# S5 mixer: states kept by pairs of groups, products of 64 rows, inputs in larger pieces, and one staging place moved

## The chip, the core and the metric

The kernel runs on one core of a Trainium2 chip. Its time is the device time of one execution in microseconds (us). Before the change three executions took 2720.01, 2723.41 and 2724.05 us; the median is 2723.41 us. Engines are named as the profile names them: PE multiplies matrices (PEld loads its weights), DVE works on vectors, ACT applies functions, POOL is a second, general vector engine, and SP issues most of the DMAs.

## What is computed

One inference step of a two-layer decoder on 1024 prompt tokens and 64 tokens of 8 samples, 1088 columns in all. Layer 0 is an S5 state-space mixer with cross-attention to a memory and a squared-ReLU MLP; layer 1 is attention with forgetting, the same memory attention and MLP. The part that is changed most is the S5 mixer: 48 groups of 16 channels, each with 64 complex states.

```python
def step(carry, u_t):                       # one chunk of 128 tokens
    hr, hi = carry
    bur = jnp.einsum("ntgc,gpc->ntgp", u_t, bb_re)
    bui = jnp.einsum("ntgc,gpc->ntgp", u_t, bb_im)
    ...
    _, _, sr, si = lax.associative_scan(_ssm_combine, (ar, ai, bur, bui), axis=1)
    y = (jnp.einsum("ntgp,gcp->ntgc", sr, c_re) - jnp.einsum("ntgp,gcp->ntgc", si, c_im)
         + d * u_t)
...
z = jax.nn.gelu(y)
out = z * jax.nn.sigmoid(z @ w_glu + b_glu)
```

The MLP is `h = relu(x @ w_up); (h * h) @ w_down` with 4096 hidden rows.

## The kernel before

Most products split a float32 operand into a rounded high part and a low part (`split`, L216: ACT copies the high part at L221, DVE or POOL subtracts it at L222) and multiply three times (`mm3`, L211). The 1088 columns are worked in four pieces of 272. Each engine works off its own queue in order; a planner that runs when the kernel is built sets the order in each queue from the order of the program and its own estimate of costs, so neighbouring parts of the program are interleaved. Memory is handed out as places that are used one after the other: `setA` (four units of 2176 words), `setB`, `setC`, and a flexible area with `sq0`, `rs0`, `nt0`. A piece of the program that writes a place waits until everyone who read it is done, DMAs too.

**Opening.** The keys and values of the memory are computed (L869 to L895; the values of one half pass through the place `u3`, from which L894 and L895 send them out), `norm0` (L905) normalizes the four pieces, where `rms_apply` (L278) gives every second split to POOL, and DVE works out the tables of S5 (L938 to L1046). ACT and POOL copy the powers of the transition matrix into `W1` and `W2`, half of the partitions at a time (L1003 to L1009).

**`prep(q)`** (L1049, six times, 8 groups each) makes the matrices of eight groups: `bb` (DVE, L1061 to L1066, 64 elements per partition), its block form `bd`, the powers `pt` (DVE, L1082 to L1087), their transposes `P` (PE, L1091), the output matrices `Q` (POOL, L1104 to L1109) and the short-range kernel, which goes through HBM and comes back as `M`.

**`phases_of(u)`** (L1131, twelve times) makes the phases by which a chunk's states are turned back and forth (DVE L1139 to L1141, POOL L1142 to L1144). **`s5_in`** (L1147) multiplies the normalized pieces with `w_in0`; the result goes through HBM and comes back as `U`.

**`s5_unit`** (L1167, twelve units of four groups): PE makes P·U in products of 64 output rows, groups 2a and 2a+1 of a pair on the lower and upper 64 partitions, real and imaginary part in separate banks. DVE multiplies by the phases (L1185, L1186), combines (L1188, L1189) and scans (L1193); POOL (L1195) and DVE (L1196) multiply the scanned states by the phases again into `A` and `B`. Then the layout changes: DVE (L1201) and POOL (L1202) assemble `Sg`, in which the 128 partitions hold the real and the imaginary states of one group. PE adds M·U and Q·Sg for each group in one bank, ACT applies Gelu (L1214), and the result goes out to HBM (L1215). The loop over units (L1225) runs nine units ahead of the dense layer of the memory queries (L1243), and the last three beside it.

**The MLP** (`mlp`, L504, once per layer) makes the hidden rows in 16 steps j; `to_hidden` (L528) combines and splits them, and SP sends them to HBM (`hops`, `hcnv`, issued at L526). Four places `hl`/`hl4` (L511, L512; for the last step L605) stage what is sent. The down product works in blocks (b, d); the first one (L639 on) writes its sums into `H5`, which lies over the same `setA` (L610): block d = 0 covers the words 0 to 1087 of each unit, block d = 1 the words 1088 to 2175. The sums are written by DVE at L627.

## Time and profile before

| | us |
|---|---|
| median of three executions | 2723.41 |
| the profiled execution | 2729.51 |
| its span, first to last instruction | 2727.7 |
| PE busy (mean granted clock 0.978) | 2564.0 |
| DVE busy | 1959.2 |
| POOL busy | 1213.1 |

The opening and the S5 mixer take the first 268 us of the span. Up to there PE is busy 213 us, DVE 233 us and POOL 163 us. The two MLPs' down products start at about 872 and 2371 us.

### The profile page before, as it was taken

Reading aid. Unit: us, or ns where it says so; the run is one execution under the profiler, and the core shown is the slowest. Engines: PE = TensorE matmul, PEld = TensorE weight load, DVE = VectorE, ACT = ScalarE, POOL = GpSimd, SP = SyncE. Lnnn points to the kernel's source line nnn. Section 1 sums busy time; section 2 is a strip of 40 time slices with the busy share of each in tenths; the row PEclk is TensorE's granted clock in tenths of the full one; section 3 lists DMA queues with packets and bytes.
Section 4 is the critical chain, followed back from the end, with each engine's and each line's share of the span. In section 5 each row is a group of like instructions: output and inputs, shape, how many; then the busy total and the mean of one; then the engine's idle time right before and its main releaser. Section 6 shows DMA issues by size and latency. Waiting matters only on the chain.

```text
span 2727.7 us, 54053 instructions
## 1 busy us (share of the span) xinstructions
PE 2564.0 (94%) x20369; PEld 2392.2 (88%) x20369; DVE 1959.2 (72%) x3406; ACT 1256.6 (46%) x2612; POOL 1213.1 (44%) x1119
## 2 busy tenths in 40 slices
PE   6888899999998999999999999999989999899998
PEld 5777779899998999999889867777989999899998
DVE  8898665988886777794323278886588788677776
ACT  5433444566663222244322367775366665322224
POOL 4576310323321799842310455651032222179984
PEclk8999899999999999999999999999999999999999
DMA  6445352266558567443476889986226656866741
GB/s 200 106 104 146 117 163 76 91 242 243 229 228 324 232 254 277 178 167 102 150 259 222 268 290 308 304 294 218 91 87 244 236 227 234 318 242 244 285 169 67
DMA packets 242283, 561.66 MB, mean 206 GB/s; under 512 B 54053, under 2 KB 129382, under 8 KB 224614
## 3 DMA queue, kind: packets, MB, share of 16 engines
q1 hardware_dynamic: 212646, 548.50, 56.7%
q10 hardware_dynamic: 28864, 8.92, 1.4%
q8 instruction: 161, 2.64, 0.4%
q0 software_dynamic: 512, 0.79, 0.1%
q14 instruction: 100, 0.82, 0.1%
HBM read 386.19 MB, written 171.93 MB: 205 GB/s over the span
## 4 chain that ended last, share of the span: by engine, by line
PE 41%; DVE 18%; POOL 10%; DMA 10%; issue 6%; ACT 4%; SPq 0%; POOLq 0%; ACTq 0%; DVEq 0%
PE banks L209 39%; DMA hops<-plain 5%; DVE rounded L222 5%; POOL plain L630 4%; DVE plain L222 4%; PE banks L1667 1%; POOL plain L416 1%; DMA rounded<-hmid 1%; DVE plain L578 1%; POOL plain L646 1%; ACT plain L221 1%; POOL plain L422 1%; DMA hcnv<-plain 1%; POOL plain L417 1%; DMA plain<-fpast 1%
## 5 line engine op out<-in xcount | busy, mean ns | idle before, releaser
L209 PE MATMUL banks<-rounded 128*128 128x272 f32 (+3 forms) x11168 | 1552.6, 295 | 72.8 <-ACT rounded L221 18.3
L209 PEld LDWEIGHTS banks<-rounded 128*128 128x128 f32 x11168 | 1456.7, 191 | 120.3 <-ACT rounded L221 21.1
L221 ACT ACTIVATE rounded<-plain 128x512 fp32r<-128x512 f32 (+5 forms) x573 | 379.8, 676 | 637.5 <-PE banks L209 449.3
L222 DVE TENSOR_TENSOR rounded<-plain,rounded 128x512 fp32r<-128x512 f32 (+4 forms) x518 | 502.8, 976 | 121.7 <-ACT rounded L221 120.3
L209 PE MATMUL banks<-mlp,rounded 128*128 128x272 f32 x3816 | 516.8, 290 | 12.2 <-DVE plain L627 4.8
L209 PEld LDWEIGHTS banks<-mlp,rounded 128*128 128x128 f32 x3816 | 493.8, 189 | 17.2 <-DVE plain L627 5.3
L416 POOL TENSOR_TENSOR plain<-plain 128x512 f32<-128x512 f32 x60 | 103.9, 1731 | 705.9 <-DVE rounded L222 705.9
L630 POOL TENSOR_TENSOR plain<-plain,flex 128x544 f32<-128x544 f32 x192 | 289.8, 1520 | 37.7 <-DVE plain L629 34.8
L222 DVE TENSOR_TENSOR plain<-plain 128x544 fp32r<-128x544 f32 x212 | 171.1, 820 | 69.9 <-ACT plain L221 69.1
L221 ACT ACTIVATE plain<-plain 128x544 fp32r<-128x544 f32 x212 | 136.7, 650 | 111.6 <-DMA hops<-plain 99.1
L629 DVE TENSOR_TENSOR plain<-banks,plain 128x544 f32<-128x544 f32 x192 | 137.9, 718 | 50.3 <-PE banks L209 46.8
L422 POOL TENSOR_TENSOR plain<-plain 128x512 f32<-128x512 f32 x60 | 98.3, 1639 | 63.0 <-DVE rounded L222 62.6
L209 PE MATMUL banks<-flexr,rounded 128*128 128x272 f32 x816 | 114.5, 290 | 4.0 <-DVE flexr L222 4.0
L209 PE MATMUL banks<-layer 128*32 128x256 f32 (+3 forms) x1152 | 111.9, 368 | 5.5 <-DVE layer L1770 1.7
L579 ACT ACTIVATE plain<-plain 128x544 f32<-128x544 f32 (+1 forms) x136 | 83.2, 613 | 66.0 <-DVE plain L578 65.5
L209 PEld LDWEIGHTS banks<-flexr,rounded 128*128 128x128 f32 x816 | 107.8, 191 | 4.4 <-DVE flexr L222 4.4
L222 POOL TENSOR_TENSOR rounded<-plain,rounded 64x512 fp32r<-64x512 f32 (+2 forms) x55 | 77.9, 1424 | 67.1 <-ACT rounded L221 61.9
L222 POOL TENSOR_TENSOR rounded<-flex,rounded 128x544 fp32r<-128x544 f32 (+7 forms) x100 | 65.9, 668 | 83.7 <-ACT rounded L221 71.0
L578 DVE TENSOR_TENSOR plain<-banks,plain 128x544 f32<-128x544 f32 (+1 forms) x136 | 90.5, 666 | 11.8 <-PE banks L209 11.2
L222 DVE TENSOR_TENSOR rounded<-banks,rounded 128x512 fp32r<-128x512 f32 (+2 forms) x136 | 86.0, 637 | 13.1 <-ACT rounded L221 11.3
L221 ACT ACTIVATE rounded<-banks 128x512 fp32r<-128x512 f32 (+2 forms) x136 | 75.1, 559 | 42.0 <-PE banks L1667 29.3
L418 POOL TENSOR_TENSOR plain<-plain 128x512 f32<-128x512 f32 x60 | 91.7, 1528 | 2.8
(365 smaller groups left out, 3227.0 us busy)
## 6 DMA issues: line engine op xcount, KB each, us to landing
hops<-plain SPq DMA_DIRECT2D x196, 544.0 KB
rounded<-hops SPq DMA_DIRECT2D x66, 1088.0 KB
plain<-in_cache_kT SPq DMA_DIRECT2D x128, 384.0 KB
layer<-in_cache_v SPq DMA_DIRECT2D x128, 384.0 KB
mlp<-hops SPq DMA_DIRECT2D x32, 1088.0 KB
plain<-in_w_up SPq DMA_DIRECT2D x32, 1024.0 KB
plain<-in_w_down SPq DMA_DIRECT2D x28, 1024.0 KB
plain<-in_xT SPq DMA_DIRECT2D x8, 1088.0 KB
```

Source lines behind the costliest of these rows:

```text
L209: PE.matmul(out, a, b, start=first, stop=last)
L221: S.activation(H, src, AF.Copy)
L222: return e.tensor_tensor(L, src, H.bitcast(F32), op=ALU.subtract)
L416: G.tensor_tensor(a22, a21, a22, op=ALU.add)
L417: G.tensor_tensor(a21, a11, a21, op=ALU.subtract)
L418: G.tensor_tensor(a11, a22, a11, op=ALU.subtract)
L422: G.tensor_tensor(a12, a12, a11, op=ALU.subtract)
L578: V.tensor_tensor(x, ps, u, op=ALU.add)
L579: S.activation(x, x, AF.Relu)
L629: V.tensor_tensor(h, ps, h, op=ALU.add)
L630: G.tensor_tensor(h, h, u, op=ALU.add)
L646: G.tensor_tensor(hc, hc, hr[:, m, :], op=ALU.add)
```

## The change

*Staging.* For the last step of an MLP the fourth staging place is words 1088 to 2175 of `setA[1]` in place of words 0 to 1087.

*Tables.* `Wr` and `Wi` hold the powers of pairs of groups, real and imaginary part apart, on all 128 partitions: 16 copies on ACT in place of 32 half ones on ACT and 32 on POOL. All of `s5_b` comes in one DMA into `u3`, and `bb` is worked out once for all six q in six DVE instructions of 384 elements. `s5_c` comes in two DMAs for each q. The phases are made for two units at a time, 512 elements per instruction. The initial states come once and are copied by ACT.

*Unit.* `Sg` is gone. DVE's last multiplication is split in two, the second one with a factor of -1. For each group PE adds M·U and four products of 64 rows: real and imaginary matrix by `B`, real and imaginary matrix by `A`; the two groups of a pair read the lower and the upper 64 partitions and write two banks. The Gelus of a unit come after all of its products.

```diff
-                hl4 = [hl.p[1], hl.p[0], hl.p[2], setA[1].sub(0, 1088)]
+                hl4 = [hl.p[1], hl.p[0], hl.p[2], setA[1].sub(1088, 1088)]
...
-    Pr, Er = late.ring(3, 1024), late.ring(3, 512)
-    abr, xring = late.ring(2, 1024), late.ring(2, 512)
+    Pr, Er = late.ring(3, 1024), Ring([late.words(1024), sq0.sub(0, 1024)])
+    abr, xring = late.ring(2, 1088), late.ring(2, 512)
...
-    W1, W2 = pp([128, 8, 48]), pp([128, 8, 48])
+    Wr, Wi = pp([128, 24, 8]), pp([128, 24, 8])
     for t in range(8):
-        for h in range(2):
-            hs = slice(64 * h, 64 * h + 64)
-            r, i = are[hs, 7 - t, :], aim[hs, 7 - t, :]
-            S.activation(W1[0:64, t, h::2], r, AF.Copy)
-            S.activation(W1[64:128, t, h::2], i, AF.Copy, scale=-1.0)
-            G.tensor_copy(W2[0:64, t, h::2], i)
-            G.tensor_copy(W2[64:128, t, h::2], r)
+        S.activation(Wr[:, :, t], are[:, 7 - t, :], AF.Copy)
+        S.activation(Wi[:, :, t], aim[:, 7 - t, :], AF.Copy)
...
+    bb = pp([128, 6, 2, 4, 16])
+    bc = u3.at([128, 6, 2, 4, 16])
+    SY.dma_start(out=bc, in_=I["s5_b"].rearrange("q p r a c -> p q r a c"))
+    tb = rs0.at([128, 6, 4, 16])
+    crb, cib = (x.rearrange("p (q a) -> p q a", a=4)[:, :, :, None].broadcast_to([128, 6, 4, 16]) for x in (cr, ci))
+    V.tensor_tensor(bb[:, :, 0], crb, bc[:, :, 0], op=ALU.mult)
+    V.tensor_tensor(tb, cib, bc[:, :, 1], op=ALU.mult)
+    V.tensor_tensor(bb[:, :, 0], bb[:, :, 0], tb, op=ALU.subtract)
...
-        bb = bbr([128, 2, 4, 16])
-        tb = tbr([128, 4, 16])
-        crb = cr[:, prs, None].broadcast_to([128, 4, 16])
-        cib = ci[:, prs, None].broadcast_to([128, 4, 16])
-        V.tensor_tensor(bb[:, 0], crb, bc[:, 0], op=ALU.mult)
-        V.tensor_tensor(tb, cib, bc[:, 1], op=ALU.mult)
-        V.tensor_tensor(bb[:, 0], bb[:, 0], tb, op=ALU.subtract)
...
+        cc = ccr([128, 2, 4, 16])
         for h in range(2):
             hs = slice(64 * h, 64 * h + 64)
-            for r in range(2):
-                S.activation(bd[64 * r:64 * r + 64, :, h, 16 * h:16 * h + 16], bb[hs, r], AF.Copy)
+            SY.dma_start(out=cc[hs], in_=I["s5_c"][q][hs].rearrange("p r (a h) c -> p h r a c", h=2)[:, h])
+            S.activation(bd[hs, :, :, 16 * h:16 * h + 16], bb[hs, q], AF.Copy)
+
+        S.activation(cc[:, 1], cc[:, 1], AF.Copy, scale=-1.0)
...
-        G.tensor_tensor(Q, wt(W1), ct(0), op=ALU.mult)
...
+            G.tensor_tensor(Q[:, i], wt(Wr), ct(i), op=ALU.mult)
             tq = tqr([128, 4, 8, 16])
-            G.tensor_tensor(tq, wt(W2)[:, gs], ct(1)[:, gs], op=ALU.mult)
-            G.tensor_tensor(Q[:, gs], Q[:, gs], tq, op=ALU.subtract)
-        S.activation(c0[0:64], cc[0:64, 0], AF.Copy)
-        S.activation(c0[64:128], cc[64:128, 1], AF.Copy, scale=-1.0)
+            G.tensor_tensor(tq, wt(Wi), ct(1 - i), op=ALU.mult)
+            G.tensor_tensor(Q[:, i], Q[:, i], tq, op=ALU.subtract if i else ALU.add)
...
-        V.tensor_tensor(B, X, Es[:, None].broadcast_to(s5b), op=ALU.mult)
-        Sg = sgr([128, 4, 136])
-        Sv = Sg.rearrange("p (a h) j -> p h a j", h=2)
+        V.tensor_tensor(B[:, 0], X[:, 0], Es, op=ALU.mult)
+        V.scalar_tensor_tensor(B[:, 1], X[:, 1], -1.0, Es, op0=ALU.mult, op1=ALU.mult)
...
+        S.activation(As[:, :, :, 128:136], hsm[:, :, 2 * u:2 * u + 2, :], AF.Copy)
+        Y = yr([128, 4, 136])
+
+        o = [ybank([128, 2, 136]) for _ in range(2)]
+        for i in range(2):
+            for h in range(2):
+                g = 4 * hh + 2 * i + h
+                mm(o[h][:, i], M[:, g, :], U[:, g, :], True, False)
+            for r, x, n, last in ((0, B[:, 1], 128, False), (1, B[:, 0], 128, False),
+                                  (0, As[:, 0], 136, False), (1, As[:, 1], 136, True)):
+                for h in range(2):
+                    hs = slice(64 * h, 64 * h + 64)
+                    mm(o[h][:, i, 0:n], Q[hs, r, 2 * hh + i], x[hs, i], False, last)
         for h in range(2):
-            hs = slice(64 * h, 64 * h + 64)
-            V.tensor_tensor(Sv[0:64, h, :, 0:128], A[hs, 0], B[hs, 1], op=ALU.subtract)
-            G.tensor_tensor(Sv[64:128, h, :, 0:128], A[hs, 1], B[hs, 0], op=ALU.add)
-        hc = slice(2 * u, 2 * u + 2)
-        G.tensor_tensor(h9[:, 0, hc, 0:1], A[:, 0, :, 127:128], B[:, 1, :, 127:128], op=ALU.subtract)
-        G.tensor_tensor(h9[:, 1, hc, 0:1], A[:, 1, :, 127:128], B[:, 0, :, 127:128], op=ALU.add)
-        S.activation(Sg[:, :, 128:136], h0[:, 4 * u:4 * u + 4, :], AF.Copy)
-        Y = yr([128, 4, 136])
-        for i in range(2):
-            ps2 = ybank([128, 272])
-            for g in (2 * i, 2 * i + 1):
-                o = ps2[:, 136 * (g % 2):136 * (g % 2) + 136]
-                mm(o, M[:, 4 * hh + g, :], U[:, 4 * hh + g, :], True, False)
-                mm(o, Q[:, 4 * hh + g, :], Sg[:, g, :], False, True)
-            S.activation(Y[:, 2 * i:2 * i + 2, :].rearrange("p b j -> p (b j)"), ps2, AF.Gelu_apprx_tanh)
+            S.activation(Y[:, h::2, :], o[h], AF.Gelu_apprx_tanh)
```

The order on DVE in the opening, in the second piece of the normalization (L272 to L285 in both; `prep_150` holds the tables, L1082 to L1087 before are the powers of `prep(0)`; L1033 and L1036 are the new instructions for `bb`, L1130 a phase). Before:

```order
104 L1063 TENSOR_TENSOR flex_69<-flex_69 128x64 [waits DVE_49]
105 L1140 TENSOR_TENSOR prep_150<-prep_150 128x256 [waits Activation_49]
106 L1065 TENSOR_TENSOR flex_69<-prep_150 128x64 [waits DVE_49]
107 L1082 TENSOR_TENSOR prep_150<-prep_150,flex_69 128x4x128
108 L1066 TENSOR_TENSOR flex_69<-flex_69 128x64 [waits DVE_49]
109 L1083 TENSOR_TENSOR prep_150<-prep_150,flex_69 128x512 [waits DVE_49]
110 L1085 TENSOR_TENSOR prep_150<-prep_150,flex_69 128x4x128
111 L1062 TENSOR_TENSOR flex_69<-prep_150 128x64 [waits DMAHW0_49]
112 L1084 TENSOR_TENSOR prep_150<-prep_150 128x4x128 [waits DVE_49]
113 L272 TENSOR_TENSOR flex_69<-flex_69 128x272 [waits Activation_49]
114 L1064 TENSOR_TENSOR flex_69<-prep_150 128x64 [waits DVE_49,Activation_49]
115 L1086 TENSOR_TENSOR prep_150<-prep_150,flex_69 128x512 [waits DVE_49]
```

After:

```order
103 L272 TENSOR_TENSOR flex_69<-flex_69 128x272 [waits Activation_49]
104 L273 SCALAR_TENSOR_TENSOR flex_69<-banks,flex_69 128x272 [waits DVE_49]
105 L274 TENSOR_SCALAR flex_69<-flex_69 128x272 [waits DVE_49]
106 L275 TENSOR_TENSOR flex_69<-flex_69 128x272 [waits DVE_49]
107 L285 SCALAR_TENSOR_TENSOR flex_69<-plain,flex_69 128x272 [waits DVE_49]
108 L285 SCALAR_TENSOR_TENSOR flex_69<-plain,flex_69 128x272 x3
109 L285 SCALAR_TENSOR_TENSOR flex_69<-plain,flex_69 128x272 [waits Pool_49]
110 L285 SCALAR_TENSOR_TENSOR flex_69<-plain,flex_69 128x272
111 L222 TENSOR_TENSOR rounded<-flex_69,rounded 128x544 [waits Activation_49]
112 L1033 TENSOR_TENSOR prep_150<-prep_150 128x6x64 [waits DMAHW0_49]
113 L1036 TENSOR_TENSOR prep_150<-prep_150 128x6x64
114 L1130 TENSOR_TENSOR plain<-prep_150 128x512 [waits DVE_49]
```

The normalization of this piece stood behind and between the instructions of `prep(0)`; these now come after all four pieces, and the piece holds the first two instructions on `bb`, which wait for a DMA.

The order on PE around the products of the first unit (64x136 is P·U; before, flex 128x136 is Q·Sg and rounded 128x136 is M·U; after, plain is Q by `B`, 128x128, and by `A`, 128x136; 128x272 is the dense layer). Before:

```order
60 L209 MATMUL banks<-rounded 128x272 x52
61 L209 MATMUL banks<-flex_69,plain 128x136
62 L209 MATMUL banks<-rounded 128x136
63 L209 MATMUL banks<-flex_69,plain 128x136 x2
64 L209 MATMUL banks<-rounded 128x136
65 L209 MATMUL banks<-flex_69,plain 128x136
66 L209 MATMUL banks<-rounded 128x272 x18
```

After:

```order
57 L209 MATMUL banks<-rounded 128x272 x32
58 L209 MATMUL banks<-plain 128x128 x4
59 L209 MATMUL banks<-plain 128x136 x4
60 L209 MATMUL banks<-rounded 128x136 x2
61 L209 MATMUL banks<-plain 128x128 x4
62 L209 MATMUL banks<-plain 128x136 x4
63 L209 MATMUL banks<-rounded 128x272 x22
```

Two products of a pair with `Sg` have become eight of 64 rows that stand in a row, and the dense layer's products follow the first unit as before.

The order on DVE at the start of the first down product of the first MLP, with what each instruction waits for (L627 writes `H5`; L445 and L449 combine sums; DMAHW are semaphores of DMAs). Before:

```order
1067 L445 TENSOR_TENSOR flex_8251<-banks,flex_8251 128x544 [waits PE_49]
1068 L222 TENSOR_TENSOR rounded<-plain,rounded 128x512 [waits Activation_49]
1069 L222 TENSOR_TENSOR rounded<-plain,rounded 128x512 [waits PE_49,Activation_49]
1070 L627 TENSOR_TENSOR plain<-banks,flex_8251 128x2x272 [waits DMAHW0_49,DVE_49]
1071 L449 TENSOR_TENSOR flex_8251<-banks,flex_8251 128x544
1072 L627 TENSOR_TENSOR plain<-banks,flex_8251 128x2x272 [waits PE_49]
1073 L627 TENSOR_TENSOR plain<-banks,flex_8251 128x2x272 [waits DMAHW1_49,DVE_49]
1074 L449 TENSOR_TENSOR flex_8251<-banks,flex_8251 128x544
1075 L627 TENSOR_TENSOR plain<-banks,flex_8251 128x2x272 [waits PE_49]
```

After:

```order
1009 L445 TENSOR_TENSOR flex_8234<-banks,flex_8234 128x544 [waits PE_49]
1010 L222 TENSOR_TENSOR rounded<-plain,rounded 128x512 [waits Activation_49]
1011 L627 TENSOR_TENSOR plain<-banks,flex_8234 128x2x272 [waits DVE_49,PE_49]
1012 L449 TENSOR_TENSOR flex_8234<-banks,flex_8234 128x544
1013 L627 TENSOR_TENSOR plain<-banks,flex_8234 128x2x272 [waits DVE_49,PE_49]
1014 L449 TENSOR_TENSOR flex_8234<-banks,flex_8234 128x544
1015 L222 TENSOR_TENSOR rounded<-plain,rounded 128x512 [waits Activation_49]
1016 L627 TENSOR_TENSOR plain<-banks,flex_8234 128x2x272 [waits PE_49] x2
```

The two writes that waited for DMAs wait for DVE and PE alone.

## Rows read from the trace of the kernel before

**Rows 1.** The page, part 4: the share of each engine on the chain that ended last.
```profile
PE 41%; DVE 18%; POOL 10%; DMA 10%; issue 6%; ACT 4%; SPq 0%; POOLq 0%; ACTq 0%; DVEq 0%
```

**Rows 2.** Busy time of each engine by stretch, up to the end of the S5 mixer. Columns: stretch, its length, then PE, PE's weight loads, DVE, ACT and POOL busy us with instruction counts, the clock granted to TensorE, the DMA share, GB/s.
```profile
50.00:70.00 20.00, 11.31 (x52) 10.10 (x52) 19.74 (x28) 6.51 (x13) 11.95 (x8) 0.60 0.19 60
70.00:112.00 42.00, 33.80 (x243) 29.57 (x243) 39.84 (x55) 19.07 (x40) 30.23 (x25) 0.96 0.29 69
...
129.00:268.00 139.00, 119.36 (x1031) 107.95 (x1030) 121.72 (x203) 44.40 (x117) 93.81 (x112) 0.96 0.46 117
```

**Rows 3.** Groups of one shape on DVE, 46 to 107 us. Columns: engine, operation, out<-in, shapes, count, busy us, mean ns of one, idle time before and what ended it.
```profile
L285 DVE SCALAR_TENSOR_TENSOR flex<-plain,flex 128x272 f32<-128x272 f32 x24 | 15.0, 682 | 0.5 <-DVE flex L275 0.5
L222 DVE TENSOR_TENSOR rounded<-flex,rounded 128x544 fp32r<-128x544 f32 x7 | 7.4, 1053 | 2.3 <-ACT rounded L221 2.3
L222 DVE TENSOR_TENSOR rounded<-plain,rounded 128x1024 fp32r<-128x1024 f32 x3 | 5.5, 1846 | 0.0
...
L272 DVE TENSOR_TENSOR flex<-flex 128x272 f32<-128x272 f32 x3 | 2.2, 738 | 0.0
...
L275 DVE TENSOR_TENSOR flex<-flex 128x272 f32<-128x272 f32 x3 | 1.6, 543 | 0.0
...
L274 DVE TENSOR_SCALAR flex<-flex 128x272 f32<-128x272 f32 x3 | 1.4, 483 | 0.0
...
L273 DVE SCALAR_TENSOR_TENSOR flex<-banks,flex 128x272 f32<-128x272 f32 x3 | 1.3, 432 | 0.0
```

**Rows 4.** Timeline of DVE from 36 to 134 us, of PE in two pieces, of the queue of SP and of POOL (columns: start, duration, engine, line, operation, out<-in, count, and in brackets the idle time before it with what ended it), and POOL's copies of the tables in 20 to 60 us, grouped as in rows 3.
```profile
52.81 2.41 DVE L1065 TENSOR_TENSOR flex<-prep 128x64 f32<-128x64 f32 x1
...
133.23 1.23 DVE L222 TENSOR_TENSOR rounded<-plain,rounded 128x1024 fp32r<-128x1024 f32 x1 [9.31 <-ACT rounded L221]
...
63.02 0.47 PE L1091 MATMUL banks<-plain,prep 128*128 128x128 f32 x1 [6.31 <-DVE prep L1084]
...
111.33 3.91 PE L209 MATMUL banks<-rounded 128*128 128x272 f32 x29 [0.97 <-POOL rounded L222]
...
116.70 12.32 PE L209 MATMUL banks<-rounded 128*128 128x272 f32 x96
128.95 1.15 PE L209 MATMUL banks<-rounded,plain 128*64 128x136 f32 x16
...
71.30 0.43 SPq L895 DMA_DIRECT2D mvscr<-prep  x1
...
109.95 1.33 POOL L222 TENSOR_TENSOR rounded<-flex,rounded 128x544 fp32r<-128x544 f32 x1
...
L1008 POOL COPY prep<-prep 64x24 f32<-64x24 f32 x16 | 6.0, 376 | 6.8 <-DVE prep L999 6.2
...
L1009 POOL COPY prep<-prep 64x24 f32<-64x24 f32 x16 | 3.3, 205 | 0.7
```

**Rows 5.** Groups of one shape, 128 to 268 us, on DVE and on POOL.
```profile
L1201 DVE TENSOR_TENSOR flex<-plain 64x256 f32<-64x256 f32 x24 | 17.8, 742 | 8.6 <-POOL plain L1195 8.3
...
L1195 POOL TENSOR_TENSOR plain<-plain 128x512 f32<-128x512 f32 x12 | 22.2, 1851 | 48.7 <-DVE plain L1193 48.7
L1202 POOL TENSOR_TENSOR flex<-plain 64x256 f32<-64x256 f32 x24 | 19.7, 820 | 2.5 <-DVE plain L1196 0.8
```

**Rows 6.** Timeline of the late units on DVE: two turns of the loop, one unit after the other, and the last Gelu of the stage on ACT.
```profile
229.68 1.71 DVE L1201 TENSOR_TENSOR flex<-plain 64x256 f32<-64x256 f32 x2 [1.18 <-POOL plain L1195]
...
238.39 1.71 DVE L1201 TENSOR_TENSOR flex<-plain 64x256 f32<-64x256 f32 x2 [1.18 <-POOL plain L1195]
...
266.49 0.67 ACT L1214 ACTIVATE flex<-banks 128x272 f32<-128x272 f32 x2
```

**Rows 7.** Timeline of PE: the last unit's products of 128 rows, with what follows (a product is two instructions).
```profile
262.55 0.50 PE L209 MATMUL banks<-flex,plain 128*128 128x136 f32 x2 [0.85 <-POOL flex L1202]
262.89 0.40 PE L209 MATMUL banks<-prep,rounded 128*128 128x136 f32 x2
263.12 0.80 PE L209 MATMUL banks<-flex,plain 128*128 128x136 f32 x4
263.76 0.40 PE L209 MATMUL banks<-prep,rounded 128*128 128x136 f32 x2
263.99 0.39 PE L209 MATMUL banks<-flex,plain 128*128 128x136 f32 x2
264.14 2.63 PE L209 MATMUL banks<-rounded 128*128 128x272 f32 x19
```

**Rows 8.** Timeline around the start of the first down product of the first MLP (SP's queue, DVE, PE), the same place on PE in the second MLP, and the stretches after the first.
```profile
857.16 7.25 SPq L526 DMA_DIRECT2D hcnv<-plain  x6
...
871.52 0.72 DVE L627 TENSOR_TENSOR plain<-banks,flex 128x544 f32<-128x544 f32 x1 [5.54 <-DMA hcnv<-plain]
...
872.93 9.24 PE L209 MATMUL banks<-rounded 128*128 128x272 f32 x53 [6.72 <-DVE flex L449]
...
2371.28 6.91 PE L209 MATMUL banks<-rounded 128*128 128x272 f32 x34 [6.79 <-DVE flex L449]
...
855.00:872.00 17.00, 8.12 (x51) 7.39 (x49) 5.82 (x10) 1.26 (x2) 1.59 (x1) 0.88 0.97 340
872.00:880.00 8.00, 7.07 (x37) 7.07 (x38) 4.83 (x8) 0.68 (x2) 0.00 (x0) 0.61 1.01 422
880.00:900.00 20.00, 20.00 (x162) 20.00 (x161) 12.18 (x18) 4.62 (x8) 4.87 (x4) 1.00 0.48 183
```

More of the change, by code (lines that the diff above doesn't have):

```diff
@@ L1169, in s5_unit @@
         P = P[:, hh].rearrange("p (a r x) -> p a r x", a=2, r=2)
-        Ec, Es = E
+        Ec, Es = (E[:, i, 2 * hh:2 * hh + 2] for i in range(2))
         o = 512 * 2
@@ L1228, in units @@
             if u == 2:
-                with after(dmas[-1]):
-                    SY.dma_start(out=h9[:, :, :, 1:9], in_=I["s5_h0p"])
-            s5_unit(q, hh, us[q], *tabs[q], es[u])
-            if u < 10:
-                es.append(phases_of(u + 2))
+                S.activation(h9[:, :, :, 1:9], hsm, AF.Copy)
+            s5_unit(q, hh, us[q], *tabs[q], es[q])
+            if hh == 0 and q < 5:
+                es.append(phases_of(q + 1))
             if hh == 0 and q < 4:
```

83 lines of the change are left out of this document (40 added, 43 removed).

## The prediction

> **What bounds the kernel now.** I read the chain of waits first: PE carries 41% of it, DVE 18%, POOL 10%, and DMAs 10% [rows 1]. PE is the bound of the kernel as a whole, so a faster DVE or POOL helps only where PE waits. The busy times by stretch show where that is. From 50 to 112 us DVE works 59.6 of 62 us while PE works 45.1; from 129 to 268 us DVE works 121.7 and PE 119.4 of 139 us, at a mean granted clock of 0.96 [rows 2]. Then I read what DVE does there. Between 46 and 107 us only 34.4 us of its 61 belong to the normalization of the input (15.0 + 7.4 + 5.5 + 2.2 + 1.6 + 1.4 + 1.3) [rows 3]; the rest, some 26 us, are tables, powers and phases that stand in its queue before the pieces. Small instructions are stretched there: a 64-element one took 2.41 us [rows 4]. PE pays with 6.31 us in which the transposes of `prep(0)` wait for DVE and with the second half of the memory's values behind them [rows 4]. In the late units the turn is 8.71 us (229.68 to 238.39), and in each one DVE stands 1.18 us before L1201 because POOL's L1195 is not done [rows 6]. The last place is the start of the down products: PE stands 6.72 us in the first MLP and 6.79 us in the second, DVE's L627 having waited 5.54 us for the stores `hcnv` [rows 8].
>
> **The change part by part.**
>
> *Staging place.* The stores that read the fourth place are issued from 857.16 on and take SP 7.25 us to issue [rows 8]; the place lies under the sums of block d = 0, so L627 waits for them until 871.52. Moved under d = 1 it is wanted only when d = 0 is done, and the order shows that the two writes wait for DVE and PE alone. PE's 6.72 us go. It also restarted at half clock: granted 0.61 in 872 to 880 us with 37 instructions in 7.07 us, 0.191 each, against 0.123 each (162 in 20.00) at clock 1.00 right after, a loss of 37 × 0.068 = 2.5 us [rows 8]. So one MLP can give 9.2 us; L445, L449 and one product still stand in a row, and some of the slow clock is already there before (0.88 in 855 to 872). I take 7.75 each, **15.5** for both. Bounds: all of it, 18; and 0 if something else is late. The DMAs are busy 0.97 and 1.01 of the time from 855 to 880 us and fall to 0.48 after it [rows 8]; what block d = 1 needs comes out of that same stretch. Without its wait L627 runs at 871.52 - 5.54 = 866.0 and PE 1.4 us later; d = 1 writes its first sums after the rest of d = 0, at least 36 products of 0.123 us, so no earlier than 867.4 + 4.4 = 871.8 us, and the stores had landed by 871.52. That is near, and it is why the low end stays.
>
> *Opening.* The 32 copies on POOL (6.0 + 3.3 us [rows 4]) and 16 of ACT's go, and in the order `prep(0)` and `prep(1)` now come after all four pieces of the normalization. Of the 26 us of other work on DVE, four phases of 512 elements, two new instructions for `bb` and the last table entries stay ahead; at about 1.0 to 1.3 us each under contention that is 7.5. So the normalization could end 19 us earlier than POOL's last split, which now ends at 109.95 + 1.33 = 111.3 [rows 4]. A new wait takes part of it: `s5_b` now comes in one load into `u3`, which the stores of the memory's values must have left; in DVE's queue its first use, L1033, stands in the middle of the second piece, and half of that piece and the two others wait behind it. The last store from `u3` was issued at 71.30 [rows 4], behind PE's 6.31 us of waiting that go; so it is issued near 65, and with the store and the load after it (an estimate, some 2 us each) `bb` can start near 69. From there half a piece and two pieces at 34.4 / 3 = 11.5 us at most, 10 with less contention, end near 95. After that PE has more to do than before: 48 products for the last piece and 96 for the third q at 12.32 / 96 = 0.128 us [rows 4], 18.5 us, and the small products of two `prep`s. For those I use the present stretch 111.3 to 128.95: 17.7 us less 125 products of 0.128 leaves 1.7 for most of one; I take 4.5 for two. First unit at 95 + 23 = 118 against 128.95: **11** us. Bounds: without the wait for `u3` the first unit would come at 115, 14 us, and somewhat more if DVE's instructions shrink to their short forms; if the load is 10 us later than I think, 1 us.
>
> *Units.* DVE loses L1201, 17.8 us, and 8.6 us of waiting; POOL loses L1202, 19.7 us [rows 5]. DVE's multiplication split in two costs nothing by itself, since the elements are the same, and with L1201 gone DVE has time to spare, 121.7 - 17.8 = 104 of 139 us. So PE becomes the bound. Its work: 119.4 us busy now; away go eight instructions with `Sg` in each of 12 units. The last unit ran 12 such instructions from 262.55 to 264.14, 0.132 each [rows 7], so 12.7 us go. New are 16 products of 64 rows, 32 instructions per unit. The trace has none; the nearest rows are the 64-column products, 16 in 1.15 us, 0.072 each, two side by side [rows 4], and the full products at 0.132 [rows 7]. Side by side it is 32 × 0.072 × 12 = 27.6 us, in turn 32 × 0.132 × 12 = 50.7. The order puts lower and upper halves in turn, into two banks, as P·U does for columns, so I take the first. About 48 dense products of the memory queries fall behind the last unit, 6.1 us, where PE waits for the next stage. A PE that no longer stops runs at clock 1.00 in place of 0.96, some 4 us. Together 119.4 - 12.7 + 27.6 - 6.1 - 4 = 124 us; with 3 to 4 us for filling and draining the stage takes 127.5 from its first product, where it took 137.5 (128.95 to the last Gelu at 266.49 [rows 6]): **10** us. If no cover were left (DVE late again by POOL's 1.85 us L1195 [rows 5] in each unit) it would be 22 less, worse than now; but DVE no longer reads what L1195 writes.
>
> The Trainium skill ("TensorE: Matmul & The Clock Gate", section "LDWEIGHTS (loading the stationary operand)") says that a weight load costs by its columns, not by its contraction rows: a load for 64 rows of 128 columns takes as long as a full one. By that alone the price of 0.132 would stand, since the 64-column products have half the load; no run here shows a 64-row load yet. It is the first rival below.
>
> *The rest* (the loads of `s5_c` in short pieces, Gelus at the end of a unit, phases in pieces of 512, `h9` by ACT instead of a DMA) lies on queues with room, SP's and ACT's; I put it at 0, and at ±2.
>
> Sum: 15.5 + 11 + 10 = 36.5. The profiled execution took 2729.5 us, so 2693; it lies 6.1 above the median of the three, so the prediction is **2687 us**. After the S5 stage and between the two MLPs the order is that of before, so gains pass through.
>
> **The rivals.**
> 1. *The 64-row products run in turn.* PE's work in the units is then 124 + 23 = 147, the stage 150.5 and term three -13: sum 13.5, **2710**. For it: nothing in the trace shows rows side by side; against it: columns are.
> 2. *The down products wait for something else.* Operands or weights of d = 1, from the full DMA queues, take the place of `hcnv`: term one falls to 0 to 5, **2700**. For it: a DMA share of 1.01; against it: the share falls to half at 880 us, when PE has taken half of d = 0.
> 3. *DVE and POOL stretch each other less.* The opening then gives 17, the units lose the 3.5 us of filling and draining, and the staging place gives its 18: 12 more, **2675**. For it: 2.41 us for 64 elements; against it: PE's own sum in the last 23 us before the first unit.
> 4. *Slower.* PE stops at each change between products of 128 and of 64 rows. There are four changes in a unit, 48 in all, on the engine that bounds the stage. With in-turn products as in 1 the sum is +13.5, so at over 0.28 us a change the kernel is slower than before, and at 0.5 us it is **2734**. The trace shows no such stop from full products to 64-column ones: the full ones end at 116.70 + 12.32 = 129.02 and the others have begun at 128.95 [rows 4].
>
> On rival 4 the Trainium skill ("TensorEngine Tiling (Array Packing)", "Key Properties") says that a change of tiling mode drains the engine. By that a stop would be seen; how long it is, the page doesn't say, and at the change of column mode in this trace none is seen.
>
> **How the numbers follow.** Forecast 0.47, with a range of its own of 2677 to 2699; rival 1 0.20, rival 2 0.13, rival 3 0.13, rival 4 0.07. 2660 to 2714 holds the forecast with both bounds of the opening, rivals 1 to 3, and leaves out rival 4 and the far ends. A measurement tells about 0.2%, 5.4 us. Slower by more needs rival 4 or several terms at their low ends: 0.07. Within it is where rivals 1 and 2 meet: 0.06. Faster: 0.87.
>
> **What would show it.** Right: no `hcnv` before L627 and PE's idle time there under 1 us; the first P·U near 118 us and the last Gelu near 245; in the late units a turn near 7 us with PE busy throughout; 32 instructions of 64 rows in about 2.3 us. Wrong: those 32 in 4 us (rival 1), a wait for `rounded<-hops` or weights in the first down block (rival 2), DVE idle before L1033 past 75 us, or PE pauses at each change of form (rival 4).

## The result and the profile after

The changed kernel takes 2700.22 us (median of four executions, 2696.61 to 2705.15), the kernel before, beside it, 2723.73 us (2720.01 to 2726.01): a ratio of 0.992, with a 95% interval of 0.9905 to 0.9935. It is 23.5 us faster. The forecast was 2687 us, a gain of 36.5; the time lies 13 us above it, inside the whole range (2660 to 2714) and 1 us outside the forecast's own (2677 to 2699). The profiled executions took 2729.51 and 2701.86 us, 27.7 us apart, some 4 us more than the medians; all times below that are read off both traces are from these two.

The page of the changed kernel, part 1 (PE's line) and part 4 (the chain by engine), against [rows 1]:

```profile
PE 2566.9 (95%) x20657; PEld 2395.4 (89%) x20657; DVE 1932.1 (72%) x3346; ACT 1247.6 (46%) x2579; POOL 1176.8 (44%) x1051
...
PE 59%; DVE 15%; POOL 10%; DMA 7%; issue 4%; ACT 3%; SPq 1%; POOLq 0%; ACTq 0%; DVEq 0%
```

PE's share of the chain rises from 41% to 59%, and those of DVE and of the DMAs fall: the waits went, and PE's own work stands in their place. Its busy time is not less (2564.0 us before). The share is no measure of the gain: by their pages it is 43% in e1 and 60% in e2 below, and e1 is the faster of the two.

**The staging place.** Timeline of the changed kernel at the start of the first down product of each MLP (columns as in [rows 8]):

```profile
851.07 10.91 PE L209 MATMUL banks<-rounded 128*128 128x272 f32 x84
...
853.02 0.72 DVE L627 TENSOR_TENSOR plain<-banks,flex 128x544 f32<-128x544 f32 x1 [0.38 <-PE banks L209]
...
854.53 0.72 DVE L627 TENSOR_TENSOR plain<-banks,flex 128x544 f32<-128x544 f32 x1 [0.16 <-PE banks L209]
...
2340.13 10.74 PE L209 MATMUL banks<-rounded 128*128 128x272 f32 x84 [0.32 <-DMA rounded<-hops]
2350.70 1.67 PE L209 MATMUL banks<-mlp,rounded 128*128 128x272 f32 x12
```

L627 waits 0.38 us for PE where it waited 5.54 for `hcnv`, and PE runs 84 products without a pause where it stood 6.72 and 6.79 us [rows 8]. Of the waits around it only PE's for the first L627, just before these rows, grew, from 2.42 to 3.23 us. The 872 and 2371 us given above as the start of the down products are where PE resumed behind its wait; the first L627 ran at 856.95 and 2355.17 us.

**The opening.** Busy time by stretch of the changed kernel (columns as in [rows 2]):

```profile
50.00:70.00 20.00, 13.74 (x78) 11.45 (x77) 16.75 (x19) 8.84 (x14) 17.72 (x13) 0.91 0.30 99
70.00:112.00 42.00, 36.72 (x260) 33.15 (x261) 37.29 (x54) 18.49 (x36) 15.08 (x12) 0.88 0.42 87
```

Timeline of the same kernel from the second piece of the normalization to the first unit (DVE, POOL, PE):

```profile
62.93 0.54 DVE L1033 TENSOR_TENSOR prep<-prep 128x384 f32<-128x384 f32 x1
63.40 0.54 DVE L1036 TENSOR_TENSOR prep<-prep 128x384 f32<-128x384 f32 x1
...
87.95 3.38 POOL L222 TENSOR_TENSOR rounded<-flex,rounded 128x544 fp32r<-128x544 f32 x2 [2.30 <-ACT rounded L221]
...
70.86 2.15 PE L209 MATMUL banks<-flex,plain 128*128 128x272 f32 x4 [4.27 <-DVE flex L273]
...
88.48 9.31 PE L209 MATMUL banks<-rounded 128*128 128x272 f32 x72 [0.30 <-ACT flex L1143]
100.34 0.33 PE L1086 MATMUL banks<-plain,prep 128*128 128x128 f32 x1 [2.55 <-DVE prep L1079]
...
118.82 1.15 PE L209 MATMUL banks<-rounded,plain 128*64 128x136 f32 x16
```

The new instructions for `bb` run at 62.93 without any wait in brackets, POOL's last split of the normalization ends at 87.95 + 3.38 = 91.3 us where it ended at 111.3 [rows 4], and the first P·U starts at 118.82 where it started at 128.95: 10.1 us earlier. Other executions with this opening have it at 118.65 to 122.44 us (e2 to e7 and e9 below), and with the old one at 127.89 and 127.96 (e1, e8).

**The units and what follows.** Busy time of the changed kernel from the first P·U to the first reduction of the memory attention (L746), and the two parts before and behind the last Gelu:

```profile
118.80:325.20 206.40, 184.24 (x1677) 165.55 (x1677) 140.97 (x264) 72.77 (x187) 103.98 (x108) 0.93 0.47 120
118.80:248.40 129.60, 122.00 (x1249) 109.17 (x1248) 96.18 (x167) 36.58 (x99) 69.54 (x78) 0.99 0.50 117
248.40:325.20 76.80, 62.23 (x429) 56.38 (x430) 44.79 (x98) 36.19 (x88) 34.44 (x30) 0.84 0.43 127
```

The same view of the kernel before:

```profile
129.00:334.70 205.70, 171.45 (x1380) 154.34 (x1380) 165.98 (x299) 75.98 (x194) 123.10 (x140) 0.92 0.45 119
129.00:266.50 137.50, 118.42 (x1027) 107.35 (x1026) 120.22 (x202) 43.52 (x115) 92.31 (x111) 0.96 0.46 114
266.50:334.70 68.20, 53.03 (x356) 46.99 (x355) 45.76 (x98) 32.47 (x81) 30.79 (x30) 0.82 0.43 130
```

The first part is 7.9 us shorter, at a granted clock of 0.99 where it was 0.96, and the last Gelu comes 18.1 us earlier (248.41 in place of 266.49 [rows 6]). The part behind it is 8.6 us longer. So at L746 the kernel is 9.5 us ahead, about as much as it was at the first unit: of the units' gain nothing is left. PE's work in the whole stretch grew by 184.24 - 171.45 = 12.8 us, and its idle time fell from 34.3 to 22.2 us, 12.1. The two cancel. Nearly all of the fall is in the first part (19.1 to 7.6); behind the last Gelu PE's idle time is as before, 15.2 and 14.6 us.

The 9.5 us lead is still there at the first L627 (847.42 against 856.95 us). At the second MLP it is 17.9 (2337.28 against 2355.17), and at the end 27.7: 8.4 and 9.8 us more behind the two waits for `hcnv`.

The first L627 is the safer mark of the two. Up to L746 the planner lets PE do more or less of other work from one kernel to the next (1195 to 1690 instructions from the first P·U on). Up to the first L627 PE does 5329 instructions in each kernel with the old units and 5617 in each with the new, and the 288 between are the 384 new less the 96 that went. From the first P·U to there it is 728.0 us before and 728.6 in the changed kernel; in e1 and e2, which up to there have the instructions of the one and of the other, it is 724.3 and 732.3. So by the traces the new units bring nothing, and the lead that is left is the opening's.

### The profile page after: what moved, and what is told of

Its sections match the earlier page's. It is cut to its first block, busy times and chain, and to the rows that moved or that the text cites. A ratio compares the mean times of both kernels' runs of the same rounds, so it can differ in the third digit from the quotient of the medians.

```text
span 2700.0 us, 54444 instructions
## 1 busy us (share of the span) xinstructions
PE 2566.9 (95%) x20657; PEld 2395.4 (89%) x20657; DVE 1932.1 (72%) x3346; ACT 1247.6 (46%) x2579; POOL 1176.8 (44%) x1051
## 4 chain that ended last, share of the span: by engine, by line
PE 59%; DVE 15%; POOL 10%; DMA 7%; issue 4%; ACT 3%; SPq 1%; POOLq 0%; ACTq 0%; DVEq 0%
PE banks L209 57%; POOL plain L630 4%; DVE rounded L222 4%; DMA hops<-plain 2%; PE banks L1658 1%; DMA rounded<-hmid 1%; POOL plain L646 1%; POOL plain L416 1%; DVE plain L222 1%; ACT rounded L221 1%; POOL plain L422 1%; POOL plain L417 1%; DVE flex L1351 1%; PE banks L801 1%; POOL plain L1284 1%
## 5 line engine op out<-in xcount | busy, mean ns | idle before, releaser
L221 ACT ACTIVATE rounded<-plain 128x512 fp32r<-128x512 f32 (+5 forms) x573 | 380.5, 678 | 646.3 <-PE banks L209 481.7
L222 DVE TENSOR_TENSOR rounded<-plain,rounded 128x512 fp32r<-128x512 f32 (+4 forms) x518 | 498.5, 967 | 128.4 <-ACT rounded L221 126.9
L209 PE MATMUL banks<-mlp,rounded 128*128 128x272 f32 x3816 | 515.9, 290 | 16.1 <-DVE plain L627 6.5
L416 POOL TENSOR_TENSOR plain<-plain 128x512 f32<-128x512 f32 x60 | 102.3, 1706 | 684.3 <-DVE rounded L222 684.3
L222 DVE TENSOR_TENSOR plain<-plain 128x544 fp32r<-128x544 f32 x212 | 172.2, 824 | 52.2 <-ACT plain L221 50.5
L221 ACT ACTIVATE plain<-plain 128x544 fp32r<-128x544 f32 x212 | 136.7, 649 | 106.7 <-DMA hops<-plain 90.5
L422 POOL TENSOR_TENSOR plain<-plain 128x512 f32<-128x512 f32 x60 | 98.7, 1645 | 63.1 <-DVE rounded L222 62.7
L222 POOL TENSOR_TENSOR rounded<-flex,rounded 128x544 fp32r<-128x544 f32 (+7 forms) x100 | 69.3, 701 | 100.2 <-ACT rounded L221 87.6
L222 POOL TENSOR_TENSOR rounded<-plain,rounded 64x512 fp32r<-64x512 f32 (+2 forms) x55 | 77.0, 1407 | 75.4 <-ACT rounded L221 70.0
L578 DVE TENSOR_TENSOR plain<-banks,plain 128x544 f32<-128x544 f32 (+1 forms) x136 | 90.6, 667 | 11.8 <-PE banks L209 10.1
L222 DVE TENSOR_TENSOR rounded<-banks,rounded 128x512 fp32r<-128x512 f32 (+2 forms) x136 | 86.0, 637 | 13.8 <-ACT rounded L221 11.8
L221 ACT ACTIVATE rounded<-banks 128x512 fp32r<-128x512 f32 (+2 forms) x136 | 75.0, 559 | 39.6 <-PE banks L1658 29.2
L209 PE MATMUL banks<-rounded,layer 128*128 128x256 f32 x480 | 89.9, 300 | 2.6 <-ACT rounded L221 1.7
```

What stands on the lines that cost most here:

```text
L209: PE.matmul(out, a, b, start=first, stop=last)
L221: S.activation(H, src, AF.Copy)
L222: return e.tensor_tensor(L, src, H.bitcast(F32), op=ALU.subtract)
L416: G.tensor_tensor(a22, a21, a22, op=ALU.add)
L422: G.tensor_tensor(a12, a12, a11, op=ALU.subtract)
L578: V.tensor_tensor(x, ps, u, op=ALU.add)
```

## The experiments

Each ran beside the kernel before on its chip. "Gain" below is (1 - ratio) times the median of before that was measured beside the run, 2722.7 to 2726.3 us; the brackets hold the 95% interval. The changed kernel's own gain, reckoned so, is 21.8 [17.7, 25.9].

**e1, the staging place alone, and e2, all but the staging place.**

e1 is the kernel before with this edit; e2 is the changed kernel with the edit undone.

```diff
-                hl4 = [hl.p[1], hl.p[0], hl.p[2], setA[1].sub(0, 1088)]
+                hl4 = [hl.p[1], hl.p[0], hl.p[2], setA[1].sub(1088, 1088)]
```

> The kernel before with the one moved staging place and nothing else. Theory (the two waits on hcnv were on the path and nothing else is late there): PE's two idle times of 6.7 us before the down products go, with the slow clock after them, 7 to 8 us each, so 2708 to 2710 us. Rival (operands or weights of the next block are late instead): 2718 to 2724 us, with a new PE wait in the first down block.

> The changed kernel with the staging place put back. Theory (the parts add up, and the opening and the mixer together give only some 8 us at the end): 2715 us, with both idle times of about 6.7 us back. Rival (the mixer's part gives nothing once the staging wait is back, since that wait absorbs it): 2722 us or more.

Measured: e1 2708.93 us, ratio 0.9935 [0.9923, 0.9947], a gain of 17.7 [14.4, 21.0]; e2 2721.9 us, 0.9985 [0.9975, 0.9996], a gain of 4.1 [1.1, 6.8]. e1 came as its theory had it. e2 came at its rival's time, but the rival's reason, that the wait for `hcnv` takes up the mixer's gain, isn't borne out: the two gains add up to the whole, so the rest of the diff brings about as much without the wait as with it. One moved place is four fifths of the result, and the rest, the opening and the units, brings about 4 us where the prediction had 21. In e2 the wait is back, on DVE and on PE:

```profile
865.70 0.72 DVE L627 TENSOR_TENSOR plain<-banks,flex 128x544 f32<-128x544 f32 x1 [5.75 <-DMA hcnv<-plain]
...
867.11 5.13 PE L209 MATMUL banks<-rounded 128*128 128x272 f32 x21 [6.93 <-DVE flex L449]
```

The trace of e1 also says how far two traces can be set against each other. Up to L746 its instructions are those of before, and it reaches L746 at 330.73 us, 3.9 us ahead of before. So a few us there are no effect; against e1 the changed kernel is 5.5 us ahead at L746, not 9.5. This view of e1 (columns as above) stands against the first lines of the two above:

```profile
127.90:330.70 202.80, 171.01 (x1380) 154.69 (x1380) 167.63 (x298) 75.69 (x193) 120.85 (x140) 0.92 0.47 121
```

PE's work grew by 13.2 us against e1 too, and its idle time fell from 31.8 to 22.2.

**e3, the 64-row products of the two halves not in turn.**

```diff
-            for r, x, n, last in ((0, B[:, 1], 128, False), (1, B[:, 0], 128, False),
...
-                for h in range(2):
-                    hs = slice(64 * h, 64 * h + 64)
+            for h in range(2):
+                hs = slice(64 * h, 64 * h + 64)
+                for r, x, n, last in ((0, B[:, 1], 128, False), (1, B[:, 0], 128, False),
...
                     mm(o[h][:, i, 0:n], Q[hs, r, 2 * hh + i], x[hs, i], False, last)
```

> The changed kernel with the 64-row products of a pair ordered so that four of the lower half are followed by four of the upper half, instead of in turn. Theory (the 16 products cost 1.1 us per run of eight because lower and upper half run side by side): a run of eight then takes 1.5 to 2.1 us, 10 to 24 us more PE work over the units, 2705 to 2718 us. Rival (the order does not matter, PE takes them side by side anyhow or the price of 0.07 us is that of a short product by itself): 2700 us and 1.1 us per run.

Measured: 2712.88 us, 0.9958 [0.9945, 0.997], a gain of 11.5 [8.2, 15.0], about 10 less than the change, as the theory had it. Timeline of PE around the first unit's products, first in the changed kernel, then in e3 (x16 joins eight products of both widths):

```profile
132.70 1.18 PE L209 MATMUL banks<-plain 64*128 64x128 f32 x16 [1.15 <-DVE plain L1188]
133.81 0.73 PE L209 MATMUL banks<-rounded 128*128 128x136 f32 x4
134.47 1.18 PE L209 MATMUL banks<-plain 64*128 64x128 f32 x16
135.58 3.02 PE L209 MATMUL banks<-rounded 128*128 128x272 f32 x22
```

```profile
133.63 1.73 PE L209 MATMUL banks<-plain 64*128 64x128 f32 x16 [0.92 <-DVE plain L1188]
135.29 0.73 PE L209 MATMUL banks<-rounded 128*128 128x136 f32 x4
135.95 1.73 PE L209 MATMUL banks<-plain 64*128 64x128 f32 x16
```

From one start to the next it is 133.81 - 132.70 = 1.11 us against 1.66. In 24 such rows that is 13.2 us. So what stands side by side is the alternation of the halves: 0.069 us an instruction with it, 0.104 without. The Trainium skill ("TensorE: Matmul & The Clock Gate", "Part 3: Packing small matmuls — row/col tiling") says that a weight load overlaps with running products only where it is for another row group; these rows agree. The same page of the Trainium skill says in "LDWEIGHTS (loading the stationary operand)" that a load costs by its columns alone. By that alone, the prediction had, the price of 0.132 would stand; it does not, since each of these instructions still loads 128 columns and they take 0.104 and 0.069.

**e4 and e6, the queries of the memory later or earlier.** The dense layer of the queries begins after 12 units, or after 6, in place of 9 (e4's edit; e6 has 6).

```diff
-QM = 9
+QM = 12
```

> The changed kernel with the whole dense layer of the memory queries behind the twelve units instead of beside the last three. Theory (after the mixer PE, ACT and POOL's queue set the pace, and the left-over query products are on the path): the last Gelu comes near 236 us, 12 us earlier, but 192 products and their evictions on ACT follow, so the gain is given back: 2698 to 2704 us. Rival (the left-over products are free, as I predicted): the whole gain passes, 2688 us.

> The changed kernel with the dense layer of the memory queries begun after the sixth unit instead of the ninth; the planner then also puts the memset of L703 and the copies of L726 ahead of the indirect loads on POOL. Theory (products left behind the units and POOL's order cost the 8.5 us that the mixer lost): no more than 20 query products follow the last Gelu, which comes 3 to 6 us later than now, and PE does not wait for the memset; 2691 to 2696 us. Rival (PE's sum alone sets the end of this stage): 2699 to 2701 us.

Measured: e4 2703.15 us, 0.9917 [0.9902, 0.9933]; e6 2699.48 us, 0.9903 [0.9881, 0.9926]. Both agree with the changed kernel within their intervals, though the last Gelu moved to 243.47 in e4 and 255.88 in e6 from 248.41. e4 has the time of its theory, though the last Gelu came 7 us later than it had it; in e6 the theory fell and the rival came. With over 100 of these products behind the last unit (e4), 71 (the changed kernel) and none (e6), the first L627 runs at 847.46, 847.42 and 847.49 us. If they filled a wait behind the units, e6 would come to it some 9 us later. So none of the three places is a free one, and the end of the units is no measure of the gain.

**e5, one memset from POOL to DVE.** Behind the units POOL issues 16 indirect loads (L1284), and in its queue the memset of `kb0` (L703), which PE waits for, stands behind 14 of them. Before, it stood behind five, and PE waited 5.46 us (at 314.36 us) for what stood behind the last one, L798. Chain of waits of the changed kernel, in order of time, at the place:

```profile
219.49 34.24 PE banks L209 x309
253.76 0.40 ACT flex L689
254.16 0.43 ACT rounded L221
254.60 1.09 DVE rounded L222
...
256.41 3.91 DMA plain<-yscr
...
266.51 3.60 DMA plain<-in_head_rows
...
294.79 1.83 POOL glu L703
```

The timeline of PE and POOL, with the 71 query products that are left behind the last unit:

```profile
248.31 9.18 PE L209 MATMUL banks<-rounded 128*128 128x272 f32 x71
...
282.33 6.34 POOL L1284 DMA_INDIRECT plain<-in_logf_rows,plain  x1 [0.31 <-issue]
288.97 0.92 POOL L1284 DMA_INDIRECT plain<-in_logf_rows,plain  x1 [0.30 <-issue]
...
298.06 1.20 PE L209 MATMUL banks<-glu 128*128 128x512 f32 x2 [8.77 <-ACT glu L221]
```

```diff
-        G.memset(kb0.at([128, 2048], F32R).bitcast(F32), 0.0)
+        V.memset(kb0.at([128, 2048], F32R).bitcast(F32), 0.0)
```

> The changed kernel with the clearing of the memory keys' block form (L703) on DVE instead of POOL, where it stands behind 14 indirect loads. Theory (PE's 8.8 us before 298 us wait for this memset, through ACT's copy): PE starts the scores some 6 to 8 us earlier and 3 to 8 us remain at the end, 2692 to 2697 us. Rival (the next thing in POOL's queue, the copies of L726 behind the last indirect load, is late by as much): 2699 to 2701 us.

Measured: 2707.36 us (2701.01 to 2714.45), 0.9926 [0.9901, 0.9952]: no gain over the changed kernel; the theory fell. The trace is of the slowest execution. The wait of 8.77 us went, and PE waited for the next thing in POOL's queue, still behind the same loads:

```profile
302.23 0.69 PE L801 MATMUL banks<-plain,glu 128*128 128x128 f32 x2 [4.34 <-POOL glu L798]
```

One instruction moved past a long queue only shows the next one behind it.

**e7, the indirect loads early, and e8, the same with the staging place alone.** The two small loads and the 16 indirect ones are put at the end of the units' loop, where POOL now has room, in place of behind the normalization.

```diff
     for _ in left:
         pass
+    SY.dma_start(out=pidx, in_=I["page_rows"])
+    SY.dma_start(out=hrow, in_=I["head_rows"])
...
+    past_rows()
...
-        if c == 2:
-            with after(gi):
-                past_rows()
```

> The changed kernel with the page and head rows loaded at once and the 16 indirect loads (L1284) issued behind the units in the program, not after the last load of the mixer's result; the planner spreads them over POOL's idle time between the last units. Theory (after the last Gelu POOL's chain, head rows, 16 indirect loads, memset, sets when memory attention starts, so a mixer that ends earlier gains little): PE's 8.8 us before 298 us go and 6 to 9 us remain at the end, 2691 to 2695 us. Rival (PE's own products and the round trip of the mixer's result set it): 2697 to 2701 us.

> The same edit on the kernel of e1 (before, with the staging place moved). It is the control: e8 less e7 is what the mixer's and the opening's part is worth when POOL's chain is out of the way, where e1 less the changed kernel is 8.7 us. Theory: 2703 to 2708 us, the part is worth 12 to 15 us. Rival: the part is worth the same 8 us, e8 some 8 us above e7 whatever that is.

Measured: e7 2693.9 us (2692.16 to 2695.63), 0.989 [0.9872, 0.9908], a gain of 29.9 [25.0, 34.8], the best of all, as the theory had it; e8 2703.27 us, 0.9927 [0.9912, 0.9941], a gain of 19.9 [16.1, 24.0]. In e7 the wait of 8.77 us is gone, and the stretch behind the last Gelu (251.72 us) is 63.9 us long with 55.25 of PE, so PE idles 8.7 us in it where it idled 14.6:

```profile
119.60:315.60 196.00, 180.34 (x1642) 161.90 (x1642) 140.60 (x263) 72.46 (x183) 98.25 (x107) 0.94 0.48 127
...
251.70:315.60 63.90, 55.25 (x393) 50.17 (x394) 43.43 (x97) 35.55 (x84) 13.93 (x13) 0.89 0.46 142
```

Moving the loads is worth 8.1 us on the changed kernel and 2.2 on e1 by gains, 6.3 and 5.7 by medians. With them out of the way units and opening together bring e8's median less e7's, measured beside each other: 9.4 us, less than the theory's 12 to 15, against 4.1 in e2 where the loads are in the way. So part of the gain of opening and units, perhaps 5 us, was lost in that queue. The intervals are too wide to call this shown. By the traces the 9.4 are the opening's: the first P·U comes at 119.62 us in e7 and at 127.96 in e8, 8.3 us later, and from there to the first L627 it is 721.6 and 722.0 us. So the units bring nothing with POOL's loads out of the way either.

**e9, e7 with the queries earlier** (`QM = 6`).

> e7 with the memory queries' dense layer begun after the sixth unit. Theory (left-over query products behind the units cost PE time that is not hidden): 3 to 6 us below e7. Rival (PE's sum up to memory attention counts, and the order within it does not): within 2 us of e7.

Measured: 2698.15 us, 0.991 [0.9892, 0.9928]: not better than e7, and 4.3 us above it, measured beside it (2695.89 to 2700.10 against 2692.16 to 2695.63). The theory fell, and the rival's 2 us are exceeded too.

**e10, `bb` in 36 small instructions.** The changed kernel with its one large load, but the six instructions of 384 elements cut into 36 of 64.

```diff
-    V.tensor_tensor(bb[:, :, 0], crb, bc[:, :, 0], op=ALU.mult)
...
+    for q in range(6):
...
+        V.tensor_tensor(bb[:, q, 0], crb, bc[:, q, 0], op=ALU.mult)
...
```

> The changed kernel with bb worked out in 36 DVE instructions of 64 elements instead of 6 of 384, at the same place in the program. Theory (the opening's 10 us come from the order, prep behind the normalization, more than from the larger pieces): the first P·U within 2 us of 118.8 and 2699 to 2702 us. Rival (the larger pieces are what shortens DVE's work there): the first P·U at 122 to 125 us, 2703 to 2707 us.

Measured: 2706.36 us, 0.9933 [0.9912, 0.9953], 3.6 us less gain than the change, as the rival had it, though the two intervals overlap. Timeline of PE, in the slowest of four executions:

```profile
76.11 6.59 PE L209 MATMUL banks<-flex,plain 128*128 128x272 f32 x16 [8.55 <-DVE prep L1039]
...
125.09 1.15 PE L209 MATMUL banks<-rounded,plain 128*64 128x136 f32 x16
```

The products of the normalization that ran at 70.86 wait until 76.11, and the first P·U comes at 125.09, 6.3 us later. A phase of 512 elements also moved ahead of that piece in DVE's queue (1.75 us), so the 6 us are those of the cut with what the planner made of it. The latest first P·U with the uncut opening is e5's, 122.44; only 2.7 us of the 6.3 lie beyond it.

**e11, the large `bb` alone on the units of before (with e1's staging place), and e12, e11 with the loads early.** One load of `s5_b` and six instructions for `bb`; tables, phases and units stay as before. Some small tables sit in other free memory to make room.

```diff
+    bc = u3.at([128, 6, 2, 4, 16])
+    SY.dma_start(out=bc, in_=I["s5_b"].rearrange("q p r a c -> p q r a c"))
...
+    V.tensor_tensor(bb[:, :, 0], crb, bc[:, :, 0], op=ALU.mult)
...
-        SY.dma_start(out=bc, in_=I["s5_b"][q])
...
-        V.tensor_tensor(bb[:, 0], crb, bc[:, 0], op=ALU.mult)
...
```

> The kernel of e1 (before, with the staging place moved), its units, matrices and phases unchanged, but with s5_b in one load and bb in six instructions of 384 elements. Theory (the opening's larger pieces give some 6 to 9 us and the new units nothing, since PE's added 13 us eat the waits they remove): the first P·U at 119 to 122 us and 2700 to 2704 us, level with the changed kernel. Rival (the new units are worth some us of their own at the end): 2705 to 2709 us.

> e11 with the row loads issued early as in e7. Theory: some 6 us below e11 as in the other two pairs, 2694 to 2699 us, level with e7 (2693.9) within 3 us. Rival (POOL's early row loads cost old units, which wait for POOL's multiplication, and new units are worth their gain): 2699 us or more.

Measured: e11 2713.95 us, 0.9958 [0.9944, 0.9973], a gain of 11.4, less than e1's 17.7; e12 2706.53 us, 0.9935 [0.9921, 0.995]. Both theories fell; e11 is slower than its rival had it too, and e12 came as its rival had it. In this third pair the early loads are worth 7.4 us by medians. Timeline of PE in e11:

```profile
107.50 2.86 PE L209 MATMUL banks<-rounded 128*128 128x272 f32 x11 [6.43 <-ACT flex L1151]
...
129.67 1.15 PE L209 MATMUL banks<-rounded,plain 128*64 128x136 f32 x16
```

POOL's last split of the normalization ends at 101.2 us, ten earlier than before, but PE then waits 6.43 us in `s5_in` and the first P·U comes no earlier. The large `bb` does not bring the gain of the opening by itself, and e10 suggests that it is needed for it. Which of the other pieces does (the 32 copies less on POOL, the phases in pieces of 512, the order of the preps) was not tried. Nor is it settled why e11 ends behind e1. That e12 reaches L746 at 313.72 us, before e8's 318.09, says nothing: PE has done 1195 instructions since the first P·U by then, and 1257 in e8. At the first L627, with the same work done, e12 is 5.0 us behind (854.94 against 849.96) and e11 7.3 behind e1 (859.43 against 852.18).

## Why the prediction was right, and where it failed

The direction and the first of the three terms were right. Of the 21 us of the other two, 4.1 [1.1, 6.8] came. The range was wide toward this side for the sake of rivals 1 and 2, and what these describe did not come: that the time lies in it, and on the 2700 of rival 2, owes something to luck.

*Staging place: right, a little small.* 15.5 was predicted, 17.7 [14.4, 21.0] measured alone, near the bound of 18 that took all of PE's idle time and the slow restart. The low end (d = 1 late) did not come; rival 2 falls, PE ran on through 84 products.

*Opening: 11 predicted, 10.1 in the trace; the place was right, its steps only in sum.* Of the 34.4 us that the prediction gave to the normalization, the 5.5 of the rows of 128x1024 are splits of weights. "`bb` can start near 69" was wrong: `s5_b` had landed and L1033 ran at 62.93 without waiting, and the normalization ended at 91.3, not "near 95". But then PE waited 2.55 us for the powers of `prep(0)` (L1079), which now stand behind the normalization on DVE, and it came to its first unit 27.5 us after that end, not 23. That two errors of about 4 us cancelled was luck. The slow small instructions were the right thing to look at, and e11 shows that to remove some of them is not enough.

*Price of the 64-row products: right.* "Side by side", 0.072, was chosen between 0.072 and 0.132; measured 0.069, and the 32 instructions of a unit take 2.2 us, where about 2.3 were forecast. Rival 1 falls. That the trace of before showed it for columns alone was the doubt, and e3 shows what the choice hung on. For rival 4 a stop at a change of form was asked for. Rows that change between 128 and 64 rows (132.70, 133.81, 134.47, 135.58) follow each other with no idle time in brackets, and the four full instructions between two runs of 64 rows take 0.66 us (133.81 to 134.47), where four in a row took 0.64 before (263.12 to 263.76 [rows 7]). That a change of mode drains the engine, as "Key Properties" in the Trainium skill's "TensorEngine Tiling (Array Packing)" says, costs nothing that these rows show.

*Units: wrong, 10 us predicted and none found.* The work on PE was right: predicted 27.6 - 12.7 = 14.9 us more, measured 12.8 to 13.2 from the first P·U to L746. The clock rose as expected (0.96 to 0.99), and the stretch to the last Gelu was 129.6 us where 127.5 was predicted, with the last four units 8.0 us apart (216.50 to 248.41) and not "near 7". What failed are two sentences: "About 48 dense products of the memory queries fall behind the last unit, 6.1 us, where PE waits for the next stage", and "the order is that of before, so gains pass through". The products did fall behind (71 from 248.31 on, 9.18 us, where 19 in 2.63 us stood [rows 7]), and they covered no wait: PE's idle time behind the last Gelu stayed (15.2 to 14.6), and it is much the same in e4 (13.8), with over 100 of them, and in e6 (15.6), with none. Why is open. In the chain of the changed kernel, PE's 309 instructions up to 253.73 are followed by the eviction of a query (ACT L689) and, behind it in ACT's queue, by a split (L221, then L222 on DVE) that the next stage's load from `yscr` waits for, so that there the end of the wait hangs on those products. No run tests that link by itself, and it is not the whole reason: in e6, where none of these products is left, 8.55 of the 15.6 us go to L798 behind POOL's loads. So the 6.1 us that I took off PE's sum were to be left in: with them the units gain 4, and not 10. A part of the rest may have gone into POOL's queue, whose order behind the units was not that of before (the memset behind 14 indirect loads in place of 5); PE waited there before too (5.46 us, now 8.77). The prediction went by the order at three places, and none of them is behind the units.

In short: the units traded some 10 to 12 us of waiting on PE for 13 us of work on PE. As POOL and DVE lost 19.7 and 17.8 us of layout work [rows 5], the trade looks good by their busy time. On the chain it was nearly even.

*What stays open.* By the traces opening and units together bring 9.5 us at L746 against before, 5.5 against e1; by the times of e2 4.1 [1.1, 6.8]. Two executions with the same instructions up to there differ by 3.9, so the share of each under 5 us is not told apart. What e7, e8 and the stretches up to the first L627 show puts all of it on the opening; no run has the whole new opening with the old units, or the reverse. Rival 3 (2675) is refuted by the sum.

## What to carry to other kernels

Work that is moved behind a stage is not free because a wait stands there: here 71 products moved and the wait stayed. Before taking such work off the sum, follow the chain from it into the next stage, through the in-order queue of the engine that evicts it, and look for another queue that sets the end of the wait. A gain must be followed to a place where every version has done the same work, not to the last instruction of the stage; here 18 us at the last Gelu were 9.5 further on. The cheapest edit, one address of a staging place under a store that is still being sent, brought four fifths of the gain, and a second small one, moving 16 loads out of a queue that PE waits for (e7, 6 to 8 us), brought about as much as the whole new mixer with its opening (4 to 9).

## What the runs showed of the hardware that I had not expected

Products of 64 rows one after the other on the same half take 0.104 us an instruction (1.66 us for 16), in turn 0.069; full ones took 0.132 in the mean [rows 7]. So even without alternation they are cheaper than full ones.

An indirect load of POOL (L1284) mostly takes 0.92 us with 0.30 before the next, but single ones took 1.36, 1.58 and 6.34 us in one profile; the last is the row at 282.33 above, and what made it long isn't seen in the trace.

DVE's instructions lengthen beside POOL's work: in the changed kernel's trace L1080, L1079, L1081 and L1082, of 512 elements, take 0.68 to 0.69 us each from 106.96 us on and 1.47 to 1.65 each from 114.24 on, when POOL works on `Q` (113.73 to 123.2).
